# Gate and value products by Strassen's scheme, over four token blocks of 264

## The chip, the cores and the metric

The kernel runs on one core of a Trainium2 chip. Its engines each follow their own instruction stream: the tensor engine (PE in the profile, with its weight loads as PEld), the vector engine (DVE), the scalar engine (ACT), GpSimd (POOL) and the sync engine (SP), whose queue issues most of the loads from memory. The metric is the device time of one execution in microseconds (us). Before the change it is 2893.56 us, the median of three runs from 2892.72 to 2894.1.

## The reference

One layer of a decoder runs over 1024 prompt tokens and 32 sample tokens (8 sequences of 4), 1056 tokens together, with a model width of 1024. A conditioning vector gives nine modulation vectors (shift, scale and gate for each of three parts). The layer is a feed-forward network, a mixer (gated delta heads beside latent attention heads), and a second feed-forward network:

```python
def swiglu_ffn(h, wi, wo):
    gate, up = jnp.split(h @ wi, 2, axis=-1)
    return (jax.nn.silu(gate) * up) @ wo
...
    h = rms_norm(x, lp['norm_ffn1']) * (1 + mods[:, 1]) + mods[:, 0]
    x = x + 0.5 * mods[:, 2] * swiglu_ffn(h, lp['ffn1_wi'], lp['ffn1_wo'])
    h = rms_norm(x, lp['norm_mix']) * (1 + mods[:, 4]) + mods[:, 3]
...
    mix = jnp.concatenate([gdn_out, mla_out.astype(gdn_out.dtype)], axis=-1) @ lp['w_out']
    x = x + mods[:, 5] * mix
    h = rms_norm(x, lp['norm_ffn2']) * (1 + mods[:, 7]) + mods[:, 6]
    x = x + 0.5 * mods[:, 8] * swiglu_ffn(h, lp['ffn2_wi'], lp['ffn2_wo'])
```

The hidden width D_FF is 2816, which is 22 tiles of 128. The matrix wi holds the gate columns and, behind them, the value columns (the second half, called "up" in the reference). All data is float32.

## The kernel before, in words

Tokens stand in the columns, features in the 128 partitions. The 1056 tokens are cut into three blocks of 352 columns; the last block ends with the 32 sample tokens. Every float32 operand of a large product is split into two parts, hi and lo, and a product is three matmuls into one accumulator (`mm3`, lines 114 to 118: weight hi by activation hi, weight hi by activation lo, weight lo by activation hi; L116, L117, L118 in the profile). The hi part is a cast on ACT (L97 for weights), the lo part a subtraction on POOL or DVE (L100).

A feed-forward network (`ffn`, L354 to L405) works in chunks of two of the 22 hidden tiles. `up` of one hidden tile loads its 128 gate columns and its 128 value columns (512 KB each, through the SP queue into three buffers `wraw`), splits them, and for each token block runs 8 steps of the inner dimension times 3 matmuls for the gate and as many for the value: 3 x 2 x 24 = 144 matmuls of 352 columns, tile `pg`, two buffers of two banks. ACT takes the silu of the gate (L373), DVE multiplies it with the value (L375), ACT casts (L377), DVE subtracts (L378): the result is `ahl`. `down` of a chunk takes 3 blocks x 8 output tiles x 6 = 144 matmuls into `po`, and DVE adds each `po`, times the gate modulation, to the resident x (`residual`, L345; for the 32 sample tokens, whose modulation differs by sequence, two more small instructions, L349 and L351, in the last block). `down` of one chunk stands between the two `up`s of the next. All weights of a network are loaded and split once.

Each engine runs its instructions in the order in which they stand in its program, and a scheduler decides that order when the kernel is built, from its own model of the times. An instruction whose input is late holds everything behind it on its engine. Split weights go through eight buffers (`w`).

`norm_apply` makes hi and lo of the normalised, modulated x for one block. `load_x` brings x in and transposes it, `ada` computes modulation vectors, and `mixer_out` is the mixer's output product, followed by the norm of the second network.

## Time and profile before

| | |
|---|---|
| time, median of three runs | 2893.56 us (2892.72 to 2894.1) |
| the profiled execution's own time | 2880.28 us |
| its span, first to last instruction | 2878.3 us |
| mean granted clock of the tensor engine | 0.971 |
| PE busy | 2745.4 us, 95% of the span |
| PEld busy | 2527.9 us, 88% |
| DVE busy | 1586.6 us, 55% |
| ACT busy | 916.9 us, 32% |
| POOL busy | 803.8 us, 28% |
| loads of wi, of wo (512 KB each) | 88, 44 |

The first network's products run from about 58 us to between 800 and 900 us of the span, the mixer from there to about 2100 us, the second network from there to the end. A busy share says how long an engine had something in work, not whether the end waited for it: the chain of waits and the stage tables of the trace tell that. Matmuls overlap in their pipeline, so the time that one costs is the distance from its start to the start of the next, not its own duration. In the rows of the trace, an instruction group stands as line, engine, operation, output<-input, shapes and count, then busy us, mean ns of one, and the idle time ahead of it with what ended it.

### The profile page before, as it was taken

What the parts mean: (1) busy time and instruction counts of PE and PEld (TensorE: products, weight loads), DVE (VectorE), ACT (ScalarE), POOL (GpSimd) and SP (SyncE); (2) the same over time, 40 slices, a digit from 0 to 9 for tenths busy, and PEclk for the clock granted to TensorE, in tenths of its full rate; (3) what the DMA queues carried; (4) which work ended last, traced back from release to release, by engine and by line L of the source; (5) the groups of instructions that cost most, each with busy time, mean ns of one, the idle gap of its engine ahead of it and who ended that gap; (6) DMA issues with size and microseconds to landing.
All of it is one profiled execution on the core that took longest, in us unless ns stands there. A gap on an engine that the chain in (4) does not pass through costs nothing.

```text
span 2878.3 us, 45708 instructions
## 1 busy us (share of the span) xinstructions
PE 2745.4 (95%) x18596; PEld 2527.9 (88%) x18596; DVE 1586.6 (55%) x3260; ACT 916.9 (32%) x1674; POOL 803.8 (28%) x624
## 2 busy tenths in 40 slices
PE   6999999999999898889999988888999999999999
PEld 4899999999998788888877866666999999999998
DVE  6233333333356669977766768887364343344445
ACT  4211111111124544426666654444241111111111
POOL 3111111111123354463443556540231111111110
PEclk7999999999999999989999999997999999999999
DMA  7432322311122384551221243313211111111111
GB/s 256 128 93 88 103 87 91 90 42 52 45 70 77 114 218 135 168 171 25 69 51 48 56 114 88 89 49 106 75 52 45 45 45 45 44 52 52 45 37 61
DMA packets 286171, 238.78 MB, mean 83 GB/s; under 512 B 89390, under 2 KB 248870, under 8 KB 285192
## 3 DMA queue, kind: packets, MB, share of 16 engines
q1 hardware_dynamic: 276408, 207.54, 24.6%
q0 software_dynamic: 6144, 20.98, 2.2%
q10 hardware_dynamic: 3408, 7.33, 0.8%
q8 instruction: 147, 2.41, 0.3%
q14 instruction: 64, 0.52, 0.1%
HBM read 192.66 MB, written 43.15 MB: 82 GB/s over the span
## 4 chain that ended last, share of the span: by engine, by line
PE 43%; DVE 7%; issue 5%; POOL 4%; DMA 2%; ACT 1%; POOLq 0%; DVEq 0%; ACTq 0%; SPq 0%
PE pg L116 6%; PE pg L118 6%; PE pg L117 6%; PE po L116 4%; PE po L117 4%; PE po L118 4%; POOL gt L1353 2%; PE kraw L116 1%; PE kraw L118 1%; PE kraw L117 1%; POOL gS L1353 1%; PE pS L116 1%; DVE kss L1829 1%; PE pS L117 1%; PE pS L118 1%
## 5 line engine op out<-in xcount | busy, mean ns | idle before, releaser
L116 PE MATMUL pg<-hhi,whi 128*128 128x352 f32 x2112 | 685.3, 325 | 1.5 <-ACT hhi L333 1.5
L118 PE MATMUL pg<-hhi,wlo 128*128 128x352 f32 x2112 | 681.3, 323 | 0.0
L117 PE MATMUL pg<-hlo,whi 128*128 128x352 f32 x2112 | 679.9, 322 | 0.2 <-POOL hlo L334 0.2
L345 DVE SCALAR_TENSOR_TENSOR x<-po,modT,x 128x352 f32<-128x352 f32 (+1 forms) x552 | 314.0, 572 | 564.6 <-PE po L118 559.9
L100 POOL TENSOR_TENSOR wlo<-wraw,whi 128x1024 fp32r<-128x1024 f32 x93 | 226.1, 2436 | 1339.1 <-ACT whi L97 1148.6
L116 PEld LDWEIGHTS pg<-hhi,whi 128*128 128x128 f32 x2112 | 397.0, 188 | 21.9 <-issue 20.1
L117 PEld LDWEIGHTS pg<-hlo,whi 128*128 128x128 f32 x2112 | 398.4, 189 | 4.0 <-issue 3.4
L118 PEld LDWEIGHTS pg<-hhi,wlo 128*128 128x128 f32 x2112 | 397.0, 188 | 1.7 <-issue 1.7
L116 PE MATMUL po<-ahl,whi 128*128 128x352 f32 x1056 | 344.1, 326 | 3.1 <-DVE rt L349 1.1
L117 PE MATMUL po<-ahl,whi 128*128 128x352 f32 x1056 | 341.1, 323 | 0.0
L118 PE MATMUL po<-ahl,wlo 128*128 128x352 f32 x1056 | 340.0, 322 | 0.0
L97 ACT CAST whi<-wraw 128x1024 fp32r<-128x1024 f32 x140 | 145.3, 1049 | 528.3 <-PE po L117 285.3
L375 DVE TENSOR_TENSOR fa<-fs,pg 128x352 f32<-128x352 f32 x132 | 68.4, 519 | 324.8 <-ACT fs L373 324.7
L1829 DVE TENSOR_REDUCE kss<-ksq 128x8 f32<-128x512 f32 x256 | 173.3, 681 | 73.8 <-ACT ksq L1828 71.8
L373 ACT ACTIVATE fs<-pg 128x352 f32<-128x352 f32 x132 | 61.0, 462 | 459.9 <-PE pg L118 459.4
L116 PEld LDWEIGHTS po<-ahl,whi 128*128 128x128 f32 x1056 | 198.5, 188 | 8.4 <-issue 3.8
L1828 ACT ACTIVATE ksq<-kraw 128x512 f32<-128x512 f32 x256 | 152.1, 598 | 159.8 <-PE kraw L118 122.2
L117 PEld LDWEIGHTS po<-ahl,whi 128*128 128x128 f32 x1056 | 200.3, 190 | 0.0
L118 PEld LDWEIGHTS po<-ahl,wlo 128*128 128x128 f32 x1056 | 199.2, 189 | 0.0
L116 PE MATMUL pp<-hhi,whi 128*128 128x352 f32 (+1 forms) x576 | 191.9, 334 | 6.0 <-ACT hhi L333 2.3
L117 PE MATMUL pp<-hlo,whi 128*128 128x352 f32 (+1 forms) x576 | 190.9, 332 | 2.5 <-DVE hlo L337 1.4
L118 PE MATMUL pp<-hhi,wlo 128*128 128x352 f32 (+1 forms) x576 | 191.7, 335 | 1.5 <-POOL tss L728 1.5
(491 smaller groups left out, 4893.4 us busy)
## 6 DMA issues: line engine op xcount, KB each, us to landing
wraw<-ffn_wi SPq DMA_DIRECT2D x88, 512.0 KB
adaw<-ada_w SPq DMA_DIRECT2D x72, 512.0 KB
wraw<-ffn_wo SPq DMA_DIRECT2D x44, 512.0 KB
wraw<-w_in SPq DMA_DIRECT2D x23, 512.0 KB
x_d<-x SPq DMA_DIRECT2D x3, 1408.0 KB
x<-x_d SPq DMA_DIRECT2D x3, 1408.0 KB
dml<-dm_d SPq DMA_DIRECT2D x8, 512.0 KB
wraw<-w_out SPq DMA_DIRECT2D x8, 512.0 KB
```

The lines of the kernel that those rows point to most:

```text
L97: nc.scalar.copy(hi, raw)
L100: eng.tensor_tensor(out=lo, in0=raw, in1=f(hi), op=ALU.subtract)
L116: nc.tensor.matmul(out, whi, ahi, start=first, stop=False)
L117: nc.tensor.matmul(out, whi, alo, start=False, stop=False)
L118: nc.tensor.matmul(out, wlo, ahi, start=False, stop=last)
L345: nc.vector.scalar_tensor_tensor(out=x[:, d, :n], in0=ps[:, :n], scalar=self.modT[:, m, d, 0:1], in1=x[:, d, :n], op0=ALU.mult, op1=ALU.add)
L373: nc.scalar.activation(s, pg[:, 0, :BW], AF.Silu)
L375: nc.vector.tensor_tensor(out=a, in0=s, in1=pg[:, 1, :BW], op=ALU.mult)
L1353: mul = lambda out, a, b, op=ALU.mult: nc.gpsimd.tensor_tensor(out=out, in0=a, in1=b, op=op)
L1828: nc.scalar.activation(sq, kr, AF.Square)
L1829: nc.vector.tensor_reduce(out=ss[:, (j * 4 + m) * H:(j * 4 + m + 1) * H], in_=sq.rearrange("p (h d) -> p h d", h=H), axis=AX.X, op=ALU.add)
```

## The change

The tokens are cut into four blocks of 264 columns. Each network runs over all hidden tiles for blocks 0 and 1, then again for blocks 2 and 3; the weights are therefore loaded, combined and split twice.

For one hidden tile and a pair of token blocks, the gate and value products are a product of 2 x 2 blocks: A11 and A12 are the gate columns for the lower and upper half of the inner dimension, A21 and A22 the value columns; B11 and B21 are the two halves of the activations of the first block, B12 and B22 those of the second. The 8 block products are replaced by the 7 of the table `PRODUCTS` (Strassen's scheme in Winograd's form), each of 4 steps times 3 matmuls: 84 matmuls of 264 columns for a hidden tile and pair. `ffn_weights` makes the seven weight forms (A11, S3, S2, A12, S1, A22, S4) from the loaded columns by four sums and seven splits: for a hidden tile and pass, 7 casts on ACT, 6 instructions of 512 elements on DVE and 5 on POOL. `operands` makes the seven activation forms of a pair from the staged, normalised x (`staged`); the forms of the second pair of the first network are made while the first pair's last two `down`s run. `ffn_up` runs the products in four PSUM banks, X, Y, Z and W, and combines them on ACT and DVE: the first product in X is copied out (s1), then X collects the fourth product too; u2 = s1 + Y, u3 = u2 + Z, and the gates and values follow. `down` takes 2 blocks x 8 x 6 = 96 matmuls of 264 columns, its `po` alternating over the tags B, Y, B, X.

The matmuls through `mm3` go from 6336 (`pg`) + 3744 (`po`) + 1728 (`pp`, the mixer's input product) = 11808 of 352 columns to 7392 (X, Y, Z, W) + 4992 + 2304 = 14688 of 264 columns. In all, DVE's instructions go from 3260 to 4213, ACT's from 1681 to 2407, POOL's from 624 to 1145; loads of wi from 88 to 176, of wo from 44 to 88. The attention's small weight `wuk` is split at the mixer's start instead of at the kernel's; x of blocks 2 and 3 comes through the SP queue.

```diff
--- before.py
+++ after.py
@@ constants @@
-NB = 3
+NB = 4
 BW = NT // NB
...
+TAGS = (("lo1", "hi2", "lo2", "hi3", "lo3", "e0", "e1"), ("hi3", "e1", "e2", "e0", "lo0", "hi0", "lo1"))
+STAGE = 60.0
+PRODUCTS = (("B11", "A11", "X", False), ("T3", "S3", "Z", False), ("T2", "S2", "Y", False), ("B21", "A12", "X", True),
+            ("T1", "S1", "W", False), ("T4", "A22", "Z", True), ("B22", "S4", "W", True))
@@ class Kernel @@
...
+    def halve(self, hi, lo, src, eng):
+        self.nc.scalar.copy(hi, src)
+        eng.tensor_tensor(out=lo, in0=src, in1=f(hi), op=ALU.subtract)
+    def staged(self, p, places, mscale, mshift, ps):
+        self.stage = {}
+        for n, (b, t) in enumerate(zip((2 * p, 2 * p + 1), places)):
+            rb = self.norm_rows(b, ps)
+            for g in range(2):
+                self.stage[f"B{g + 1}{n + 1}"] = t[:, g]
+                self.normed(t[:, g], b, g, rb, mscale, mshift)
+                yield
+    def operands(self, tags):
+        nc = self.nc
+        F = self.forms = {x: self.slot(t, [P, 2, 4, BW], F32R, x) for (x, *_), t in zip(PRODUCTS, tags)}
+        q = self.stage
+        def done(n, at, eng):
+            self.halve(F[n][:, 0], F[n][:, 1], q[at], eng)
+        def minus(out, a, b):
+            nc.vector.tensor_tensor(out=q[out], in0=q[a], in1=q[b], op=ALU.subtract)
+        done("B11", "B11", nc.vector)
+        yield
+        minus("B11", "B12", "B11")
+        minus("B12", "B22", "B12")
+        yield
+        done("T3", "B12", nc.gpsimd)
+        yield
+        minus("B12", "B22", "B11")
+        yield
+        done("T2", "B12", nc.vector)
+        yield
+        done("B21", "B21", nc.gpsimd)
+        yield
+        minus("B21", "B21", "B12")
+        yield
+        done("T1", "B11", nc.vector)
+        yield
+        done("T4", "B21", nc.gpsimd)
+        yield
+        done("B22", "B22", nc.vector)
+        yield
 
...
-    def ffn(self, wi, wo, mgate, tp, ps, each, hook=lambda us: None, banks="B"):
+    def ffn_weights(self, wi, ff):
+        nc = self.nc
+        F = wi.shape[1] // 2
+        g = self.load_cols(wi, ff * P, P)
+        u = self.load_cols(wi, F + ff * P, P)
+        A11, A12, A21, A22 = g[:, 0:4], g[:, 4:8], u[:, 0:4], u[:, 4:8]
+        W = {}
+        def part(n, src, eng):
+            t = W[n] = self.wsp.tile([P, 2, 4, P], F32R, tag="w", name=n, bufs=self.wbufs)
+            self.halve(t[:, 0], t[:, 1], src, eng)
+        def tt(eng, out, a, b, op=ALU.subtract):
+            eng.tensor_tensor(out=out, in0=a, in1=b, op=op)
+        part("A11", A11, nc.gpsimd)
+        tt(nc.vector, A21, A11, A21)
+        part("S3", A21, nc.vector)
+        tt(nc.vector, A21, A22, A21)
+        part("S2", A21, nc.vector)
+        part("A12", A12, nc.gpsimd)
+        tt(nc.gpsimd, A11, A21, A11, ALU.add)
+        part("S1", A11, nc.gpsimd)
+        part("A22", A22, nc.gpsimd)
+        tt(nc.vector, A12, A12, A21)
+        part("S4", A12, nc.vector)
+        return W
+    def ffn_up(self, W, act, tp, ps, hook):
+        nc = self.nc
+        B = {n: ps.tile([P, 512], F32, tag=n, name="p" + n)[:, 0:BW] for n in "XZYW"}
+        T = lambda n, w, bufs: tp.tile([P, w], F32, tag=n, name=n, bufs=bufs)
+        tt = lambda out, a, b, op=ALU.add: nc.vector.tensor_tensor(out=out, in0=a, in1=b, op=op)
+        sg, cc = T("sg", 2 * BW, 2), T("cc", 2 * BW, 2)
+        for n, (x, w, bank, add) in enumerate(PRODUCTS):
+            for k in range(4):
+                self.mm3(B[bank], W[w][:, 0, k], W[w][:, 1, k], self.forms[x][:, 0, k], self.forms[x][:, 1, k], k == 0 and not add, k == 3 and (add or bank == "Y"),
+                         skip_group_check=True)
+            if n == 0:
+                s1 = T("s1", BW, 1)
+                nc.scalar.copy(s1, B["X"])
+            elif n == 2:
+                u2, u3 = T("u2", BW, 2), T("u3", BW, 2)
+                tt(u2, s1, B["Y"])
+                tt(u3, u2, B["Z"])
+            elif n == 3:
+                nc.scalar.activation(sg[:, :BW], B["X"], AF.Silu)
+            elif n == 4:
+                tt(cc[:, BW:], u3, B["W"])
+            elif n == 5:
+                tt(cc[:, :BW], u2, B["Z"])
+            elif n == 6:
+                tt(u3, u2, B["W"])
+                nc.scalar.activation(sg[:, BW:], u3, AF.Silu)
+            hook(1.45)
+        tt(cc, sg, cc, ALU.mult)
+        nc.scalar.copy(act[:, 0], cc)
+        nc.gpsimd.tensor_tensor(out=act[:, 1], in0=cc, in1=f(act[:, 0]), op=ALU.subtract)
+    def ffn(self, wi, wo, mgate, tp, ps, acts, tags, each, late, hook=lambda us: None, banks="B"):
 
         nc = self.nc
         nf = wo.shape[0] // P
...
+        turn, self.wcount = 0, 0
+        chunks = [range(c, min(c + CH, nf)) for c in range(0, nf, CH)]
+        def down(p, chunk, act, each=None, side=None):
+            ws = [self.split(self.load_rows(wo, ff * P), (D,)) for ff in chunk]
+            for b in (2 * p, 2 * p + 1):
+                c = slice(b % 2 * BW, b % 2 * BW + BW)
                 for d in range(KT):
                     po = ps.tile([P, 512], F32, tag=banks[d % len(banks)], name="po")
-                    for n, (ff, act) in enumerate(chunk):
+                    for n in range(len(chunk)):
                         self.mm3(po[:, :BW], ws[n][0][:, d * P:(d + 1) * P], ws[n][1][:, d * P:(d + 1) * P],
-                                 act[b][:, 0], act[b][:, 1], n == 0, n == len(chunk) - 1)
+                                 act[:, n, 0, c], act[:, n, 1, c], n == 0, n == len(chunk) - 1)
                     self.residual(b, d, mgate, po, tp)
-                    hook(0.45 * len(chunk))
-                    if last:
+                    hook(0.36 * len(chunk))
+                    if each:
                         each(b, d)
...
+        for p in range(2):
+            prev = None
+            for c in chunks:
+                act = self.slot(acts[turn % 2], [P, CH, 2, 2 * BW], F32R, "act")
+                turn += 1
+                last = c is chunks[-1]
+                self.ffn_up(self.ffn_weights(wi, c[0]), act[:, 0], tp, ps, hook)
+                if prev and not last:
+                    down(p, *prev)
+                for n, ff in enumerate(c[1:]):
+                    self.ffn_up(self.ffn_weights(wi, ff), act[:, 1 + n], tp, ps, hook)
+                if last:
+                    side = late() if p else self.operands(tags)
+                    down(p, *prev, side=side)
+                    down(p, c, act, each, side)
+                    for _ in side:
+                        pass
+                prev = c, act
 
@@ def mixer_out @@
-        for b in range(NB):
...
+        side = iter(())
+        for p in range(2):
             for n, w in enumerate(ws):
-                product(b, KT - 3 + n, w)
-                self.norm_squares(b, tn, *((KT - 4, 2), (KT - 2, 1), (KT - 1, 1))[n], nc.vector)
-                if b and n == 0:
-                    self.norm_sums([b - 1], tn, ps)
-                    self.norm_apply(b - 1, 7, 6, tn, ps, NB - 1)
-        self.norm_sums([NB - 1], tn, ps)
-        self.norm_apply(NB - 1, 7, 6, tn, ps, NB - 1)
+            self.norm_sums([2 * p, 2 * p + 1], tn, ps)
+            if not p:
+                side = operands()
+        for _ in side:
+            pass
@@ def body @@
...
+    def banks(e, name):
+        pool = lambda t, n: e.enter_context(tc.tile_pool(reuse_waits="tile", name=name + t, bufs=n, space=PSUM))
+        return Banks(**{t: pool(t, n) for t, n in (("X", 1), ("Y", 1), ("Z", 1), ("W", 1), ("B", 2), ("C", 2))})
...
+                    k.load_x((0, 1), ("hi0", "lo0", "hi1"), ps, nc.scalar)
+                    k.small_vectors(tp, ps, "C")
+                    for b in (0, 1):
+                        k.norm_squares(b, tn, eng=(nc.gpsimd, nc.vector)[b])
+                    k.norm_sums((0, 1), tn, ps)
+                    k.key_tables(tp, ps, "C")
+                    run(k.ada(0, 2, tp, ps, "C", ("lo1", "hi2", "lo2", "hi3", "lo3", "e0", "e1", "e2")))
+                    run(k.staged(0, places("lo0", "hi1"), 1, 0, ps))
+                    run(k.operands(TAGS[0]))
+                    k.load_x((2, 3), ("hi0", "e2", "lo0"), ps, nc.sync)
...
+                        for b in (2, 3):
+                            k.norm_squares(b, tn)
+                            yield
+                        k.norm_sums((2, 3), tn, ps)
+                        yield from k.staged(1, places("lo0", "hi1"), 1, 0, ps)
+                        for m in (3, 5, 7):
...
-                        k.ffn(ins["ffn1_wi"][0], ins["ffn1_wo"][0], 2, tp, ps, each, hook)
+                    k.ffn(ins["ffn1_wi"][0], ins["ffn1_wo"][0], 2, tp, ps, ("e2", "hi0"), TAGS[0], each, late, hook, "BYBX")
...
+                    bg, credit = k.staged(1, places("hi2", "lo3"), 7, 6, ps), [0.0]
-                    k.ffn(ins["ffn2_wi"][0], ins["ffn2_wo"][0], 8, tp, ps, finished, banks=POT[0])
+                    k.ffn(ins["ffn2_wi"][0], ins["ffn2_wo"][0], 8, tp, ps, ("hi1", "lo2"), TAGS[1], finished, lambda: iter(()), hook, "BYBX")```

DVE in the second network before, around the end of an `up` and the start of a `down` (fa and ahl are the products of an `up`, x0 is token block 0, wlo a split weight):

```order
L375 TENSOR_TENSOR fa_26955<-fs_26953,pg_26904 128x352 [waits Activation_49]
L378 TENSOR_TENSOR ahl_26957<-fa_26955,ahl_26957 128x352 [waits Activation_49]
L345 SCALAR_TENSOR_TENSOR x0_20194<-po_27028,modT_62,x0_20194 128x352 [waits PE_49]
L100 TENSOR_TENSOR wlo_27253<-wraw_27250,whi_27252 128x1024 [waits DMAHW6_49,Activation_49]
L375 TENSOR_TENSOR fa_27011<-fs_27009,pg_26960 128x352 [waits Activation_49]
L345 SCALAR_TENSOR_TENSOR x0_20194<-po_27036,modT_62,x0_20194 128x352 [waits PE_49]
```

DVE after, at the same kind of place, first pass of the second network (wraw_27026 is the value column block of the next hidden tile, DMAHW a load's semaphore):

```order
L447 TENSOR_TENSOR u3_26825<-u2_26824,pW_26783 128x264 [waits DVE_49,PE_49]
L428 TENSOR_TENSOR wraw_27026<-wraw_27024,wraw_27026 128x512 [waits DMAHW6_49,DMAHW7_49,DMAHW4_49,Pool_49]
L447 TENSOR_TENSOR cc_26785<-sg_26784,cc_26785 128x528 [waits Activation_49]
L405 SCALAR_TENSOR_TENSOR x0_23649<-po_26896,modT_62,x0_23649 128x264 [waits PE_49]
L405 SCALAR_TENSOR_TENSOR x0_23649<-po_26904,modT_62,x0_23649 128x264 [waits PE_49]
L405 SCALAR_TENSOR_TENSOR x0_23649<-po_26912,modT_62,x0_23649 128x264 [waits PE_49]
L405 SCALAR_TENSOR_TENSOR x0_23649<-po_26920,modT_62,x0_23649 128x264 [waits PE_49]
L340 TENSOR_TENSOR S3_27032<-wraw_27026,S3_27032 128x512 [waits Activation_49]
```

Before, a weight's lo part stood between residuals; now the first sum of the next hidden tile's weights, which waits for loads and for POOL, stands ahead of the multiplication that ends the `up` and of the residuals of `down`.

PE after, between the products of one hidden tile (tile X takes B11 by A11, then B21 by A12, then Z takes T4 by A22), in the order that 36 of the 88 `up`s have; in the others between 12 and 36 matmuls of other products stand between the two products in X:

```order
L117 MATMUL pX_33052<-B11_29072,A11_33027 128x264
L118 MATMUL pX_33052<-B11_29072,A11_33027 128x264
L116 MATMUL pX_33052<-B21_29075,A12_33038 128x264 [waits Activation_49]
L117 MATMUL pX_33052<-B21_29075,A12_33038 128x264
...
L118 MATMUL pX_33052<-B21_29075,A12_33038 128x264
L116 MATMUL pZ_33053<-T4_29077,A22_33045 128x264 [waits DVE_49]
```

Before, the two accumulations of `pg` had no instruction of another engine between them; now the second product in X waits for ACT's copy of the first.

POOL after, around the change from one hidden tile's weights to the next (act is the lo part of an `up`'s result):

```order
L340 TENSOR_TENSOR A22_27046<-wraw_27026,A22_27046 128x512 [waits Activation_49]
L340 TENSOR_TENSOR A11_27162<-wraw_27158,A11_27162 128x512 [waits DMAHW0_49,Activation_49]
L428 TENSOR_TENSOR wraw_27158<-wraw_27160,wraw_27158 128x512 [waits DMAHW1_49,DMAHW5_49,DVE_49,Pool_49]
L340 TENSOR_TENSOR A12_27173<-wraw_27158,A12_27173 128x512 [waits PE_49,Activation_49]
L340 TENSOR_TENSOR S1_27177<-wraw_27158,S1_27177 128x512 [waits PE_49,Activation_49]
L340 TENSOR_TENSOR A22_27180<-wraw_27160,A22_27180 128x512 [waits PE_49,Activation_49]
L472 TENSOR_TENSOR act_26750<-cc_27058,act_26750 128x528 [waits Activation_49]
```

POOL's sum in place (L428) waits for DVE's subtraction from the same buffer, and the lo part that `down` needs (act) stands behind the five weight instructions.

321 lines of the change are left out of this document (144 added, 177 removed).

## The prediction

> **What bounds the kernel now.** I read the page first: busy shares, the chain of waits, and the costliest groups.
>
> ```profile
> PE 2745.4 (95%) x18596; PEld 2527.9 (88%) x18596; DVE 1586.6 (55%) x3260; ACT 916.9 (32%) x1674; POOL 803.8 (28%) x624
> ...
> PE 43%; DVE 7%; issue 5%; POOL 4%; DMA 2%; ACT 1%; POOLq 0%; DVEq 0%; ACTq 0%; SPq 0%
> ...
> L116 PE MATMUL pg<-hhi,whi 128*128 128x352 f32 x2112 | 685.3, 325 | 1.5 <-ACT hhi L333 1.5
> ...
> L345 DVE SCALAR_TENSOR_TENSOR x<-po,modT,x 128x352 f32<-128x352 f32 (+1 forms) x552 | 314.0, 572 | 564.6 <-PE po L118 559.9
> L100 POOL TENSOR_TENSOR wlo<-wraw,whi 128x1024 fp32r<-128x1024 f32 x93 | 226.1, 2436 | 1339.1 <-ACT whi L97 1148.6
> ```
>
> PE has hardly any idle time ahead of its gate and value products (1.5 us in 2112), while DVE waits 564.6 us for `po` and POOL 1339.1 us mostly for ACT's casts. Then the stage tables (columns: stretch, its length, busy time and count of PE, PEld, DVE, ACT, POOL, granted clock, DMA share, GB/s):
>
> ```profile
> 2300.00:2500.00 200.00, 200.00 (x1256) 200.00 (x1255) 83.63 (x160) 34.15 (x52) 28.70 (x12) 1.00 0.15 46
> ...
> 780.00:900.00 120.00, 111.81 (x679) 105.31 (x678) 75.32 (x178) 39.40 (x66) 37.44 (x30) 0.97 0.26 83
> 900.00:1000.00 100.00, 94.56 (x587) 86.87 (x585) 55.82 (x119) 44.28 (x93) 33.92 (x28) 1.00 0.25 75
> ```
>
> Inside a network PE is never idle: 200.00 / 1256 = 159.2 ns for each matmul of 352 columns, and this alone sets the time. The change gains what its matmuls take less, and loses every wait that it gives PE.
>
> **a. The matmuls.** No row has 264 columns. The nearest are the attention's:
>
> ```profile
> 1652.58 0.28 PE L117 MATMUL pa<-plo,vhi 128*128 128x128 f32 x1
> 1652.69 0.28 PE L118 MATMUL pa<-phi,vlo 128*128 128x128 f32 x1
> ...
> 1652.97 0.28 PE L117 MATMUL pa<-plo,vhi 128*128 128x256 f32 x1
> 1653.09 0.28 PE L118 MATMUL pa<-phi,vlo 128*128 128x256 f32 x1
> 1653.21 0.28 PE L116 MATMUL pT<-qk,qk 104*128 104x256 f32 x1
> ```
>
> From start to start, 256 columns take 0.12 us, and 128 columns 0.11, a floor. Between 256 and 352 columns the slope is (159.2 - 120) / 96 = 0.41 ns a column, so 264 take about 0.121 (0.119 to 0.124, since the rows have two digits). 14688 x 0.121 = 1777 us replace 11808 x 0.1592 = 1880: **-103** (-132 to -59). By parts: `up` 7392 x 0.121 - 6336 x 0.1592 = -114, `po` (`down` and the mixer's output) 4992 against 3744 = +8, the mixer's input 2304 against 1728 = +4, since a narrower matmul costs a little more for each column. The Trainium skill (TensorE: Matmul & The Clock Gate, Back-to-back issue gap) gives an isolated gap of columns / 2.4 + 2.5 ns; that would be an estimated 112.5 ns at 264 and a gain of 228 us, but the same formula has 149 ns at 352, where the trace has 159.2.
>
> I call one `down` and two `up`s of a pair a **round**: 264 x 0.121 = 31.9 us of PE; the same share of work takes 34.4 before (216 x 0.1592). There are 44 rounds, 40 of them with a `down` between `up`s.
>
> **b. The copy of X.** In 36 of 88 `up`s the second product in X follows directly on the first, and waits until ACT has copied it.
>
> ```profile
> 2410.51 0.32 PE L118 MATMUL pg<-hhi,wlo 128*128 128x352 f32 x1
> 2410.93 0.47 ACT L373 ACTIVATE fs<-pg 128x352 f32<-128x352 f32 x1 [0.30 <-PE pg L118]
> ...
> 2419.61 0.49 ACT L377 CAST ahl<-fa 128x352 fp32r<-128x352 f32 x1 [0.59 <-DVE fa L375]
> ...
> 2420.13 0.52 DVE L378 TENSOR_TENSOR ahl<-fa,ahl 128x352 fp32r<-128x352 f32 x1 [0.55 <-ACT ahl L377]
> ...
> L373 ACT ACTIVATE fs<-pg 128x352 f32<-128x352 f32 x132 | 61.0, 462 | 459.9 <-PE pg L118 459.4
> L1524 ACT ACTIVATE pf<-pT 128x512 f32<-128x512 f32 x48 | 28.5, 598 | 15.5 <-PE pT L118 11.5 <-DVE qk L1467 2.1 <-POOL plo L1528 1.8
> ```
>
> ACT starts 0.10 us after a matmul ends (2410.83 to 2410.93), and the next engine 0.03 us after ACT (2420.10 to 2420.13). A matmul of 264 columns ends about 0.28 us after its start, 0.16 later than its successor could begin; the copy takes 0.462 - 88 x 0.00085 = 0.39 us; with both handovers that is 0.68 us, times 36 = **+25** (14, if only the copy counts, to 25). In the other `up`s, 12 or more matmuls (1.45 us) lie between.
>
> **c. Weights late at the start of a `down`.** Weight work doubles, and per hidden tile it is now a chain over three engines:
>
> ```profile
> 363.26 0.38 SPq L106 DMA_DIRECT2D wraw<-ffn_wi  x1
> ...
> 367.13 1.05 ACT L97 CAST whi<-wraw 128x1024 fp32r<-128x1024 f32 x1 [2.98 <-DMA wraw<-ffn_wi]
> ...
> L1528 POOL TENSOR_TENSOR plo<-pf,phi 128x512 fp32r<-128x512 f32 x48 | 61.9, 1295 | 102.4 <-ACT phi L1527 94.6 <-PE pss L118 6.1 <-PE pT L1522 1.2
> L1527 ACT CAST phi<-pf 128x512 fp32r<-128x512 f32 x48 | 29.8, 622 | 0.9
> L1808 DVE TENSOR_TENSOR klo<-kpt,khi 128x512 fp32r<-128x512 f32 x64 | 43.8, 685 | 6.6 <-ACT khi L1807 6.0
> ```
>
> A load takes 3.8 us from issue to use; an instruction of 512 elements 1.30 us on POOL, 0.62 on ACT, 0.69 on DVE. Three `wraw` buffers turn: the value columns of a tile go where the tile before had its gate columns, free only when that tile's S4 is split, and S4's own `w` buffer comes free only when the `down` ends. Counted from that end:
>
> - S4 split: three casts and a subtraction behind them, 2.9 us;
> - load 3.8;
> - on DVE and ACT the difference, S3's cast and subtraction, the next difference: 0.69 + 0.62 + 0.69 + 0.69 = 2.7;
> - POOL's run, its sum and the lo parts of A12, S1 and A22 (4 x 1.30), act (528 elements, 1.33) and one wo (L100, 2.44): 9.0;
> - the next load into the buffer that this wo had: 3.8;
> - DVE's difference on it, which stands ahead of the multiplication and the residuals of the next `down`: 0.7, then 1.2 until the first residual is done.
>
> This is 24.1 us. PE meanwhile has two `up`s (20.3) and the four `po` buffers of the new `down` (4 x 0.73 = 2.9): 23.2. So PE waits 0.9 us, if nothing meets. But DVE and POOL disturb each other:
>
> ```profile
> 2413.20 1.72 DVE L378 TENSOR_TENSOR ahl<-fa,ahl 128x352 fp32r<-128x352 f32 x1 [0.55 <-ACT ahl L377]
> ...
> 2409.76 4.76 POOL L100 TENSOR_TENSOR wlo<-wraw,whi 128x1024 fp32r<-128x1024 f32 x2 [30.05 <-ACT whi L97]
> ```
>
> The same instruction takes 1.72 us beside a running POOL instruction, and 0.52 without (b's row). One such meeting in the chain (1.2 us, of which waits for ACT cover some 0.4) makes 1.7 us: x 40 = **+68**. None and a faster load (0) to more than two meetings (3.5) gives 0 to 140. What covers the chain is PE's own work; without that cover the chain would cost all of its 24 us a round.
>
> **d. The samples' block.** In the second pass DVE does three instructions for each `po` of the last block:
>
> ```profile
> 2403.51 0.55 DVE L345 SCALAR_TENSOR_TENSOR x<-po,modT,x 128x320 f32<-128x320 f32 x1
> ...
> 2404.47 0.55 DVE L345 SCALAR_TENSOR_TENSOR x<-po,modT,x 128x320 f32<-128x320 f32 x1
> ...
> L345 DVE SCALAR_TENSOR_TENSOR x<-po,modT,x 128x352 f32<-128x352 f32 x368 | 212.9, 583 | 427.6 <-PE po L118 427.5
> L345 DVE SCALAR_TENSOR_TENSOR x<-po,modT,x 128x320 f32<-128x320 f32 x184 | 101.1, 550 | 137.0 <-PE po L118 132.4
> L351 DVE TENSOR_TENSOR x<-x,rt 128x32 f32<-128x32 f32 x184 | 71.4, 390 | 5.1
> ```
>
> The three repeat every 0.96 us at 320 columns, so about 0.87 at 232 (1.03 ns a column from the two L345 rows), against PE's 0.73 for a `po`; before, PE had 0.96 too. L351 takes 390 ns on the mean, because it meets POOL; with POOL about twice as busy I add 0.4 for each. Eight `po`s fall behind by 8 x 0.54 = 4.3 us; four buffers hide 2.9, and the one that PE waits for takes its own 0.4: 1.8 us, x 20 `down`s = **+36** (0, if POOL is quiet then, to 20 x 4.0 = 80).
>
> **e. Edges.** At the change of pair DVE has eight instructions of 1056 elements for the new forms (8 x 1.4 from L1808 scaled) and 32 residuals (32 x 0.49): 27 us, against 192 matmuls = 23.2 us: +5 in each network with the first product's wait. At the start and behind the mixer's output I put 5 and 6 for the forms that PE waits for, and 4 for norms in shorter pieces: **+25** (0 to 50). PE's start is already loose, as this row shows:
>
> ```profile
> 0.00:58.00 58.00, 35.56 (x188) 18.84 (x188) 31.07 (x59) 18.80 (x24) 20.26 (x21) 0.71 0.89 299
> ```
>
> **Sum:** -103 + 25 + 68 + 36 + 25 = **+51**, on the profiled execution's 2880.28: 2931. That execution lies 13.3 us below the median of the runs, so the forecast is **2945 us**.
>
> **Rivals.** R1, *the weights come in time*: c and d vanish, -103 + 25 + 25 = -53, 2841 us, faster. For it: POOL now works 28.7 of 200 us in a network, and c without a meeting is only 0.9 us, d without POOL's meetings nothing. Against it: POOL's work per round rises to 10 x 1.30 + 2 x 1.33 + 1.33 x 2.44 = 18.9 us of 32. It decides below 53 / 40 = 1.3 us for a round, c and d together.
>
> R2, *DVE becomes the bound*, by these rows and L345's:
>
> ```profile
> L375 DVE TENSOR_TENSOR fa<-fs,pg 128x352 f32<-128x352 f32 x132 | 68.4, 519 | 324.8 <-ACT fs L373 324.7
> L100 DVE TENSOR_TENSOR wlo<-wraw,whi 128x1024 fp32r<-128x1024 f32 x47 | 57.4, 1220 | 42.1 <-ACT whi L97 41.9
> ```
>
> Per round 16 residuals x 0.49 = 7.9, ten sums of 264 x 0.43 and two products of 528 x 0.70 = 5.7, twelve weight instructions x 0.69 = 8.3, two thirds of one wo at 1.22 = 0.8: 22.7 us, and for the samples 8 x 0.37 in the second pass, 1.5 on the mean. Of these, 14.7 have both inputs in SBUF; if four in five of them wait 1.2 us for POOL, that is 14.1 more, 38.3 us a round against 34.4: 44 x 3.9 + 25 = +197, **3090 us**; it decides from about half of them on. That DVE can starve for longer is in the trace:
>
> ```profile
> 1639.29 3.91 DVE L531 TENSOR_TENSOR pv<-rsk 128x128 f32<-128x128 f32 x1
> ...
> 1639.13 1.43 POOL L1500 TENSOR_TENSOR mix<-rl,rc 64x352 f32<-64x352 f32 x2
> 1640.52 2.53 POOL L1528 TENSOR_TENSOR plo<-pf,phi 128x512 fp32r<-128x512 f32 x2
> ```
>
> Against it: ten of the sums read PSUM and L375, which reads PSUM, shows no such wait in its mean of 519 ns. The Trainium skill (SBUF — State Buffer, Who interferes with whom) says that only a DVE instruction with two SBUF inputs contends with a GpSimd instruction that reads SBUF, and that the later one blocks entirely; the 1.72 us agrees.
>
> R3, *PE's clock*: short waits in each round lower the granted clock to the 0.97 of the stretch from 780 to 900 us: 1405 x 0.03 = +42, **2987 us**. Against it: from 900 to 1000 us PE was idle for 5% and kept 1.00. [...]
>
> **Chances.** Forecast 0.44 (its own range 2895 to 3000), R1 0.33, R2 0.08, R3 0.09, and 0.06 for a balance within 0.2%, about what a measurement of this kernel can tell from no change. Faster 0.34 (R1 and a tail), same 0.06, slower 0.60. The range takes in most of R1 and R3 and leaves R2 out: 2825 to 3030.
>
> **What would show it.** a: starts 0.12 us apart within a product. b: idle ahead of PE's X products, released by ACT's copy, 36 times about 0.6 us. c: idle ahead of `po` products released by DVE's residual, behind a DVE difference that a load released. d: the same in the second pass only, with L351's successor stretched. R2 would show DVE busy for over 90% of a round, R3 a granted clock under 1.00 within a network. I am wrong if PE is idle for less than 1.2 us a round (then faster), or if the matmuls stand 0.13 us apart (then 132 us slower than summed).

## The result and the profile after

After the change the kernel takes 3214.27 us (median of four runs, 3210.24 to 3222.25) for 2893.83 us before (median of four runs beside them, 2892.72 to 2894.65): a ratio of 1.1111, 95% interval 1.1085 to 1.1137. The forecast was 2945 us with a range to 3030: the sign was right, the size far off. The profiled execution took 3210.26 us, its span is 3208.5 us, 330.2 longer than before.

The page of the kernel after: busy shares, the chain by engine, and the groups of the weights' work on POOL and DVE.

```profile
PE 2802.3 (87%) x21560; PEld 2532.0 (79%) x21560; DVE 2244.0 (70%) x4212; ACT 1286.6 (40%) x2399; POOL 1544.9 (48%) x1143
...
PE 32%; DVE 26%; DMA 15%; POOL 13%; issue 9%; ACT 5%; SPq 0%; DVEq 0%; ACTq 0%; POOLq 0%
...
L340 POOL TENSOR_TENSOR A<-wraw,A 128x512 fp32r<-128x512 f32 x264 | 407.3, 1546 | 308.7 <-ACT A L339 301.1
...
L428 DVE TENSOR_TENSOR wraw<-wraw 128x512 f32<-128x512 f32 x264 | 276.8, 1048 | 198.8 <-DMA wraw<-ffn_wi 163.0
...
L340 DVE TENSOR_TENSOR S<-wraw,S 128x512 fp32r<-128x512 f32 x264 | 266.6, 1010 | 58.5 <-ACT S L339 57.7
...
L428 POOL TENSOR_TENSOR wraw<-wraw 128x512 f32<-128x512 f32 x88 | 114.4, 1300 | 353.5 <-DVE wraw L428 288.8
```

PE is no longer the chain: DVE, loads and POOL together hold 54% of it, 13% before. POOL's lo parts of the A forms take 1.55 us where 1.30 was summed (its sum takes the 1.30), and DVE's weight instructions 1.05 and 1.01 where 0.69 was. DVE waits 163 us for loads of wi.

Where the time went, by stage. The bounds are starts of matmuls in the trace: the first product of a network, its last `po`, the last `pp` of the mixer's input, the first and last `po` of the mixer's output. All in us.

| | start | network 1 | mixer input | heads | mixer output | network 2 | tail | span |
|---|---|---|---|---|---|---|---|---|
| before | 57.9 | 814.6 | 410.5 | 722.3 | 96.3 | 769.5 | 7.1 | 2878.3 |
| after | 92.2 | 901.1 | 446.2 | 741.1 | 99.8 | 915.3 | 12.8 | 3208.5 |
| difference | 34.3 | 86.5 | 35.7 | 18.8 | 3.5 | 145.8 | 5.7 | 330.2 |

Each network has a steady part and edges. This table gives the time from start to start of a network's matmuls, in ns for each (bare, as in undisturbed stretches: 159.2 before, 121.5 after), for the first 5% of them, the next 40%, the middle 10% (the change of pair after), the next 40% and the last 5%.

| | first 5% | 40% | middle 10% | 40% | last 5% |
|---|---|---|---|---|---|
| before, network 1 | 200 | 173 | 173 | 162 | 199 |
| before, network 2 | 171 | 160 | 160 | 160 | 198 |
| after, network 1 | 142 | 160 | 189 | 141 | 177 |
| after, network 2 | 232 | 144 | 226 | 143 | 169 |

The stage table of the kernel after, for a steady stretch of network 2 (stretch, length, PE, PEld, DVE, ACT, POOL with counts, granted clock, DMA share, GB/s):

```profile
2380.00:2460.00 80.00, 70.55 (x534) 67.20 (x532) 53.82 (x83) 26.66 (x49) 43.58 (x27) 0.98 0.27 80
```

No engine is full: PE is idle for 9.45 of 80 us, DVE works 67%, POOL 54%. The limit is a chain that goes from one to the other. This is it, the chain of waits of 2400 to 2480 us, in order of time (start, length, what):

```profile
2402.00 0.61 DVE wraw L428
2402.74 1.15 POOL wraw L428
2403.99 0.75 POOL A L340
...
2405.70 1.36 POOL S L340
...
2407.42 1.75 POOL A L340
2409.17 1.74 POOL act L472
2410.91 2.36 POOL wlo L100
2413.29 4.58 DMA wraw<-ffn_wi
2417.99 0.93 DVE wraw L428
2418.98 0.63 ACT S L339
2419.65 0.59 PE pZ L116
...
2433.51 1.38 DVE S L340
2434.95 3.98 DMA wraw<-ffn_wi
2439.05 0.70 DVE wraw L428
...
2443.96 1.79 DVE cc L447
2445.76 1.71 DVE wraw L428
...
2449.51 1.94 DVE wlo L100
2451.47 5.41 DMA wraw<-ffn_wi
2456.98 1.78 DVE wraw L428
```

It is the chain that term c described, link by link: sum, POOL's run, act, wo, the load into the freed buffer, DVE's difference. But POOL's run from 2402.74 to 2413.27 takes 10.5 us for 9.0, the loads 4.0 to 5.4 for 3.8, and DVE's difference up to 1.8 for 0.7. PE meets it at two places, at the residuals and at `pZ`, the product with S3. Its waits in network 1, then in network 2 (line, what it waited for: us, times, longest):

```profile
PE po L116 <- DVE x L405: 31.0, 15, 5.9
...
PE pZ L116 <- ACT S L339: 7.2, 4, 2.5
```

```profile
PE pZ L116 <- ACT S L339: 25.8, 15, 2.2
PE po L116 <- DVE x L405: 17.6, 9, 11.2
```

### The profile page after: what moved, and what is told of

It reads as the page before. It is cut to its first block, busy times and chain, and to the rows that moved or that the text cites. A ratio compares the mean times of both kernels' runs of the same rounds, so it can differ in the third digit from the quotient of the medians.

```text
span 3208.5 us, 54936 instructions
## 1 busy us (share of the span) xinstructions
PE 2802.3 (87%) x21560; PEld 2532.0 (79%) x21560; DVE 2244.0 (70%) x4212; ACT 1286.6 (40%) x2399; POOL 1544.9 (48%) x1143
## 4 chain that ended last, share of the span: by engine, by line
PE 32%; DVE 26%; DMA 15%; POOL 13%; issue 9%; ACT 5%; SPq 0%; DVEq 0%; ACTq 0%; POOLq 0%
DMA wraw<-ffn_wi 10%; DVE wraw L428 5%; PE po L116 4%; PE po L117 4%; PE po L118 3%; DVE S L340 3%; POOL A L340 3%; POOL wlo L100 2%; ACT S L339 2%; DVE cc L447 2%; POOL gt L1449 2%; POOL wraw L428 1%; DVE cy L820 1%; PE pp L116 1%; PE pp L118 1%
## 5 line engine op out<-in xcount | busy, mean ns | idle before, releaser
L340 POOL TENSOR_TENSOR A<-wraw,A 128x512 fp32r<-128x512 f32 x264 | 407.3, 1546 | 308.7 <-ACT A L339 301.1
L116 PE MATMUL po<-act,whi 128*128 128x264 f32 x1408 | 419.5, 303 | 65.6 <-DVE x L405 48.6
L405 DVE SCALAR_TENSOR_TENSOR x<-po,modT,x 128x264 f32<-128x264 f32 (+1 forms) x736 | 334.7, 477 | 136.5 <-PE po L118 134.5
L339 ACT CAST S<-wraw 128x512 fp32r<-128x512 f32 x352 | 218.2, 620 | 512.6 <-DVE wraw L428 426.7
L428 DVE TENSOR_TENSOR wraw<-wraw 128x512 f32<-128x512 f32 x264 | 276.8, 1048 | 198.8 <-DMA wraw<-ffn_wi 163.0
L118 PE MATMUL po<-act,wlo 128*128 128x264 f32 x1408 | 394.4, 295 | 20.2 <-POOL wlo L100 16.9
L117 PE MATMUL po<-act,whi 128*128 128x264 f32 x1408 | 407.3, 293 | 0.0
L116 PEld LDWEIGHTS po<-act,whi 128*128 128x128 f32 x1408 | 277.2, 197 | 98.3 <-DVE x L405 64.2
L340 DVE TENSOR_TENSOR S<-wraw,S 128x512 fp32r<-128x512 f32 x264 | 266.6, 1010 | 58.5 <-ACT S L339 57.7
L118 PEld LDWEIGHTS po<-act,wlo 128*128 128x128 f32 x1408 | 269.6, 198 | 28.0 <-POOL wlo L100 22.9
L428 POOL TENSOR_TENSOR wraw<-wraw 128x512 f32<-128x512 f32 x88 | 114.4, 1300 | 353.5 <-DVE wraw L428 288.8
L117 PEld LDWEIGHTS po<-act,whi 128*128 128x128 f32 x1408 | 276.7, 197 | 0.0
L339 ACT CAST A<-wraw 128x512 fp32r<-128x512 f32 x264 | 162.9, 617 | 264.4 <-PE po L117 121.0
L116 PE MATMUL pX<-B,A 128*128 128x264 f32 x704 | 209.3, 297 | 42.9 <-ACT s L455 20.4
L100 POOL TENSOR_TENSOR wlo<-wraw,whi 128x1024 fp32r<-128x1024 f32 x63 | 159.8, 2538 | 152.9 <-ACT whi L97 147.3
L117 PE MATMUL pp<-hlo,whi 128*128 128x264 f32 (+1 forms) x768 | 226.3, 295 | 3.7 <-DVE hlo L340 3.7
L116 PE MATMUL pp<-hhi,whi 128*128 128x264 f32 (+1 forms) x768 | 226.9, 296 | 2.0 <-ACT hhi L339 2.0
L118 PE MATMUL pp<-hhi,wlo 128*128 128x264 f32 (+1 forms) x768 | 224.2, 293 | 0.4 <-POOL wlo L581 0.4
L118 PE MATMUL pX<-B,A 128*128 128x264 f32 x704 | 203.1, 288 | 1.2 <-POOL A L340 1.2
L117 PE MATMUL pX<-B,A 128*128 128x264 f32 x704 | 203.3, 289 | 0.3 <-DVE B L340 0.3
```

What stands on the lines that cost most here:

```text
L100: eng.tensor_tensor(out=lo, in0=raw, in1=f(hi), op=ALU.subtract)
L116: nc.tensor.matmul(out, whi, ahi, start=first, stop=False, **kw)
L117: nc.tensor.matmul(out, whi, alo, start=False, stop=False, **kw)
L118: nc.tensor.matmul(out, wlo, ahi, start=False, stop=last, **kw)
L339: self.nc.scalar.copy(hi, src)
L340: eng.tensor_tensor(out=lo, in0=src, in1=f(hi), op=ALU.subtract)
```

## The experiments

Each kernel was timed once, in the execution that was profiled, except the last; the kernel before took 2891 to 2904 us beside them. Stages in us from the traces:

| | start | network 1 | mixer, three stages | network 2 | tail | span |
|---|---|---|---|---|---|---|
| before | 57.9 | 814.6 | 1229.1 | 769.5 | 7.1 | 2878.3 |
| four blocks, no Strassen, one pass | 68.4 | 829.5 | 1268.0 | 802.6 | 6.6 | 2975.2 |
| two passes, no Strassen | 78.9 | 818.7 | 1280.0 | 798.7 | 13.3 | 2989.5 |
| after | 92.2 | 901.1 | 1287.1 | 915.3 | 12.8 | 3208.5 |
| POOL's lo parts left out | 88.6 | 810.0 | 1274.7 | 796.1 | 12.9 | 2982.2 |
| five load buffers in network 2 | 91.8 | 897.5 | 1285.7 | 829.9 | 10.9 | 3115.7 |
| ten split buffers in network 2 | 91.8 | 903.3 | 1299.3 | 852.2 | 12.8 | 3159.5 |
| POOL's weight work on DVE | 92.2 | 823.9 | 1293.0 | 811.6 | 12.7 | 3033.4 |
| the same, and five load buffers | 92.7 | 823.3 | 1277.4 | 793.9 | 11.1 | 2998.5 |
| lo parts left out, five load buffers | 87.5 | 810.3 | 1278.4 | 784.6 | 11.1 | 2971.8 |
| four forms made for seven | 76.7 | 895.5 | 1293.9 | 896.8 | 12.7 | 3175.6 |
| POOL's weight and form work on DVE | 91.4 | 822.7 | 1284.2 | 811.6 | 12.8 | 3022.8 |
| the same, and five load buffers | 90.6 | 825.0 | 1277.7 | 791.1 | 11.3 | 2995.7 |

The mixer tells how far one execution can be trusted: of the edits of the kernel after, the nine that keep Strassen leave the mixer's own instructions as they are, and it took 1274.7 to 1299.3 us in them. Differences of some 12 us in a mixer, or in a span, are not taken for effects here.

**Strassen alone undone.**

```diff
+PLAIN = (("B11", "A11", "X", False), ("B21", "A12", "X", True), ("B12", "A11", "Z", False), ("B22", "A12", "Z", True),
+         ("B11", "A21", "Y", False), ("B21", "A22", "Y", True), ("B12", "A21", "W", False), ("B22", "A22", "W", True))
...
         part("A11", A11, nc.gpsimd)
-        tt(nc.vector, A21, A11, A21)
-        part("S3", A21, nc.vector)
...
+        part("A12", A12, nc.vector)
+        part("A21", A21, nc.gpsimd)
+        part("A22", A22, nc.vector)
```

> Strassen alone is undone: four blocks of 264 and two passes stay, but a hidden tile and pair takes the eight plain block products (96 matmuls for 84), its weights are split in four halves without sums, and the activation forms are four for seven. Theory 1 (the chain that makes the seven weight forms, loads and two engines in turn, is what PE waits for): the chain is short here, so the networks take little more than their matmuls, 12672 x 0.122 = 1546 us and about 100 at the edges, for 1816 after: a span of about 3040 us. Rival (loading and splitting all weights twice is the cost, with or without sums): the networks stay at 1800 us or more, a span of 3200 us.

The span is 2989.5 us: 219 less, with 1056 matmuls more. A steady stretch of its network 2:

```profile
2300.00:2400.00 100.00, 100.00 (x825) 100.00 (x825) 41.04 (x69) 27.84 (x48) 34.50 (x22) 1.00 0.31 96
```

PE is never idle and the clock is 1.00, at 100.00 / 825 = 121.2 ns for each matmul. So in this stretch, weights that are loaded and split twice cost nothing, and 264 columns take what the forecast said; both networks together take 1617 us, 15 less than with four blocks and one pass (below). The rival falls; what costs is Strassen's own work, on the forms of weights and activations and on the sums of the products, which this run undoes all at once. Against this kernel, Strassen saves 1056 x 0.1215 = 128 us of matmuls and is 219 us slower, so it pays 347 us, 327 of them in the networks.

**POOL's lo parts of weights left out.**

```diff
         def part(n, src, eng):
...
-            self.halve(t[:, 0], t[:, 1], src, eng)
+            if eng is nc.gpsimd:
+                nc.scalar.copy(t[:, 0], src)
+            else:
+                self.halve(t[:, 0], t[:, 1], src, eng)
...
-                self.mm3(B[bank], W[w][:, 0, k], W[w][:, 1, k], self.forms[x][:, 0, k], self.forms[x][:, 1, k], k == 0 and not add, k == 3 and (add or bank == "Y"),
+                self.mm3(B[bank], W[w][:, 0, k], W[w][:, int(w in ('S2', 'S3', 'S4')), k], self.forms[x][:, 0, k], self.forms[x][:, 1, k], k == 0 and not add, k == 3 and (add or bank == "Y"),
```

> The four lo parts of weights that POOL makes for each hidden tile (A11, A12, S1, A22) are left out, and the hi part is multiplied in their place; all matmuls, loads, casts and DVE's instructions stay. Theory 1 (chain): POOL's run between two loads loses 4 x 1.5 us, so the steady rounds fall from 38.3 us to about 33. Theory 2 (DVE and POOL disturb each other): DVE's weight instructions fall from a mean of 1.05 us toward 0.69. If both hold, the networks lose some 200 of 1816 us, a span of about 3000 us; if neither is the cause (PE's rate or DVE's own work), the span stays above 3150 us.

The networks lose 210 of 1816 us, as expected if both theories hold: four instructions of a hidden tile are worth 60% of the 347 us. DVE's weight instructions fall from 1.05 and 1.01 us to 0.77 and 0.86, not all the way to 0.69; POOL's sum, act and wo are left. How much is POOL's shorter run and how much the disturbance, this run does not tell.

**Five load buffers in the second network.**

```diff
-        self.wraw = e.enter_context(self.tc.tile_pool(reuse_waits="tile", name="wraw", bufs=3))
+        self.wraw = e.enter_context(self.tc.tile_pool(reuse_waits="tile", name="wraw", bufs=raw))
...
-        with k.weights(), k.residents(), k.extra(), ExitStack() as pse:
+        with k.weights(5, 8), k.residents(), k.extra(), ExitStack() as pse:
```

> In the second network alone there are five buffers for loaded weights, not three. Theory 1 with the loads as its core: the value columns of the next tiles need not wait for the tile before, the 85 us that DVE waits for loads there mostly vanish, and the second network goes from 915 us to about 850. Theory 2 (disturbance between DVE and POOL) or a bound by their work: 915 us less 15 at most. The first network and the mixer stay.

Network 2 goes from 915.3 to 829.9 us, with every instruction of the engines kept. The waits of DVE in network 2, after and here (engine, line, what it waited for: us, times, longest):

```profile
DVE wraw L428 <- DMA wraw<-ffn_wi: 84.6, 40, 9.0
```

```profile
DVE wraw L429 <- DMA wraw<-ffn_wi: 49.2, 30, 7.4
```

85 us come back, as expected if the loads are at the core. The wait for loads does not vanish, and loads of wi still hold 100 us of network 2's chain of waits, for 182 in the kernel after. The first network keeps its three buffers, and stays (897.5 us for 901.1).

**Four blocks alone.** The kernel before with `NB = 4`, and only what four blocks need to fit.

```diff
-NB = 3
+NB = 4
...
-            for cb, n in ((0, P), (P, P), (2 * P, BW - 2 * P)):
+            for cb, n in ((0, 88), (88, 88), (176, 88)):
```

> The kernel before with four blocks of 264 for three of 352, and nothing else of the change: one pass, plain products, weights loaded and split once. By term a the networks take 12672 x 0.122 = 1546 us for 1584 before (with waits), the mixer 8 more. Theory 3 (the mixer's 55 us and the later start come from the narrower blocks, whose pieces cost DVE more): the mixer goes from 1229 to about 1280 us here too. Rival (they come from the staged forms, the order of loads and the split of wuk at the mixer's start): the mixer stays within 15 us of before, and the first product starts near 58 us.

The mixer takes 1268 us, 39 more, and the span is 96.9 us longer than before. Theory 3 holds as far as one execution can tell: most of the mixer's 58 us come with the narrower blocks (the start gives 10). PE's waits in the mixer's input, before, here, and after:

```profile
PE pch L758 <- DVE tok L742: 6.0, 2, 4.4
```

```profile
PE pch L758 <- DVE tok L742: 26.1, 6, 7.2
```

```profile
PE pch L861 <- DVE tok L845: 24.1, 6, 6.2
```

The waits for DVE's `tok` grow fourfold with the narrower blocks alone. More work on DVE is not the reason: it has 16 `tok` instructions in both kernels and is busy for 318 us of the mixer's input, 322 before. Why they come later for PE stays open.

**POOL's five weight instructions on DVE**, in both networks: `nc.vector` for `nc.gpsimd` in the four `part`s and the one sum.

```diff
-        part("A11", A11, nc.gpsimd)
+        part("A11", A11, nc.vector)
...
-        tt(nc.gpsimd, A11, A21, A11, ALU.add)
+        tt(nc.vector, A11, A21, A11, ALU.add)
```

> POOL's five instructions for the weights of a hidden tile (the lo parts of A11, A12, S1, A22 and the sum for S1) are done by DVE; POOL keeps act and two thirds of wo. Theory 2 (DVE and POOL disturb each other) and theory 1 (POOL's run lies in the chain): DVE's weight instructions fall from 1.05 us to about 0.7, five instructions of 0.7 replace a run of five of 1.5, and the networks fall from 1816 us by 100 or more. Rival (DVE is the bound): its work per round rises from about 27 us, stretched, to 31 unstretched against 32 of PE, DVE is busy over 95% of a round, and the networks stay at 1800 us or more.

The networks fall by 181 us, although DVE has 440 instructions more. The groups in network 2 of the kernel after, then of this one from 2280 us on, 71 us behind the network's start (busy, mean ns):

```profile
L428 DVE TENSOR_TENSOR wraw<-wraw 128x512 f32<-128x512 f32 x129 | 138.8, 1076 | 99.0 <-DMA wraw<-ffn_wi 84.6 <-POOL A L340 10.5 <-POOL wlo L100 3.5
...
L340 DVE TENSOR_TENSOR S<-wraw,S 128x512 fp32r<-128x512 f32 x130 | 136.7, 1052 | 33.7 <-ACT S L339 33.6
...
L405 DVE SCALAR_TENSOR_TENSOR x<-po,modT,x 128x264 f32<-128x264 f32 x264 | 119.4, 484 | 33.2 <-PE po L118 32.9
...
L411 DVE TENSOR_TENSOR x<-x,rt 128x32 f32<-128x32 f32 x88 | 24.6, 281 | 1.1
```

```profile
L340 DVE TENSOR_TENSOR S<-wraw,S 128x512 fp32r<-128x512 f32 x161 | 113.4, 704 | 10.5 <-ACT S L339 9.4
L405 DVE SCALAR_TENSOR_TENSOR x<-po,modT,x 128x264 f32<-128x264 f32 x252 | 113.3, 484 | 11.7 <-PE po L118 11.2
L428 DVE TENSOR_TENSOR wraw<-wraw 128x512 f32<-128x512 f32 x160 | 112.6, 703 | 32.7 <-DMA wraw<-ffn_wi 30.8
...
L340 DVE TENSOR_TENSOR A<-wraw,A 128x512 fp32r<-128x512 f32 x120 | 89.3, 744 | 31.2 <-ACT A L339 30.8
```

The same instructions take 0.70 us where they took 1.05 to 1.08, while the residual, which reads PSUM, takes 484 ns in both. So the 0.35 us are the disturbance by POOL. What it is worth, this run does not part from the shorter run (five instructions of 0.7 for five of 1.5): both go at once. The Trainium skill (SBUF — State Buffer, Who interferes with whom) names two SBUF inputs as the condition for a DVE instruction outside its 2-port perf modes, and the two groups agree.

**Ten split buffers, and two combinations.** `k.weights(3, 10)` in the second network; then DVE for POOL with five load buffers; then the lo parts left out with five load buffers.

> In the second network alone ten buffers for split weights stand in place of eight, the loads keep their three. If the chain is held where S4's split waits for a split buffer that comes free at the end of a down, the second network falls from 915 us to under 880; if the chain is held by the three load buffers alone, it stays within 15 us of 915.

> POOL's five weight instructions on DVE in both networks, and five load buffers in the second. The second network took 830 us with five buffers alone. If what is left there is the disturbance between DVE and POOL, it falls to about 780 us; if DVE's own work is then the limit, it stays at 830 or rises. The first network should repeat the run without the buffers.

> POOL's four lo parts are left out (the hi part is multiplied in their place) in both networks, and five load buffers in the second. Alone these gave 796 and 830 us for the second network, from 915. If POOL's run and the loads are parts of one chain, either one frees it and both together give about 785 us; if they are two separate waits, the gains add to about 711, which is close to the bare matmuls (5808 x 0.1215 = 706).

Ten split buffers alone bring network 2 to 852.2, 63 us less: the wait for a split buffer, S4's among them, is a link of the chain as well. The combinations reach 793.9 and 784.6 us, not the 726 and 711 of added gains: POOL's run and the load buffers are links of one chain, and to slacken either frees much of it. The split buffers were not tried together with another. The first combination expected about 780 and is nearer to that than to 830.

**The activation forms.** Four splits and no sums in `operands`, the products with T1 to T4 taking B12's split; and, in the next run, POOL's three form splits on DVE in addition to its weight work.

> The work on the activation forms is cut to that of the plain products: four splits (B11, B12, B21, B22) and no sums; the products with T1 to T4 take B12's split in their place. Weights, matmuls and everything else stay. After the change, the middle tenth of a network's matmuls (the change of pair) took 226 ns for each in the second network and 189 in the first, for 121.5 bare. If the forms' work on DVE and POOL is what PE waits for there, this falls to about 160, and the first product starts some 8 us earlier: together about 65 us less, a span near 3145 us. Rival (stores of y that hold load buffers, and the weights' fresh start): the middle tenth stays over 205 ns and the span within 25 us of 3208.

> As the run with POOL's five weight instructions on DVE, and POOL's three lo parts of activation forms on DVE too. If the disturbance between the two engines also holds up the change of pair, whose instructions of 1056 elements took 3.4 us on DVE for 1.4 expected, the middle tenth falls from 178 ns (second network) and 151 (first) toward 150 and 135, about 25 us in all, a span near 3010 us. If DVE's own added work cancels it, the span stays within 10 us of 3033.

The start comes 15.5 us earlier, but the middle tenth of network 2 only falls from 226 to 205 ns (of network 1 from 189 to 171), and the span by 33 us, half of what was expected. To move the form splits from POOL makes no difference that one run can show (3022.8 for 3033.4, network 2 the same 811.6, the middle tenths 180 and 153 ns for 178 and 151), though the splits of T then take DVE 1.3 to 1.4 us. So the forms are a part of the cost of a change of pair, and not its larger one. The rest shows two waits: in the kernel after, DVE first waits behind POOL (first two fences: timeline of DVE and of POOL), and then the second pass's first weights wait for the stores of y, which use the load buffers (third: chain of waits):

```profile
2707.03 3.38 DVE L377 TENSOR_TENSOR st<-st 128x1056 f32<-128x1056 f32 x1 [1.64 <-POOL T L340]
2710.34 3.40 DVE L340 TENSOR_TENSOR B<-st,B 128x1056 fp32r<-128x1056 f32 x1
```

```profile
2703.55 3.44 POOL L340 TENSOR_TENSOR T<-st,T 128x1056 fp32r<-128x1056 f32 x1
```

```profile
2750.84 5.23 DMA y_prompt<-yt
2756.21 5.88 DMA wraw<-ffn_wi
2762.21 0.70 DVE wraw L428
```

With five load buffers the middle tenth of network 2 was 181 ns, which fits the rival, but with POOL's lo parts left out it was 173 and with POOL's weight work on DVE 178, with three load buffers. So the weights' chain is in it too; how the rest divides was not tried.

**All three together**, with two timed runs.

> All three changes that freed the chain together: POOL's weight and form work on DVE, five load buffers in the second network. By the single runs the span is about 2975 us. It stays slower than the kernel before, because four narrow blocks alone cost 97 us (span 2975 without Strassen) and the bare matmuls that Strassen saves against plain products are 1056 x 0.1215 = 128 us, of which the copies of X, the forms and the clock take back about that much. Rival: with the chain freed, Strassen's 128 us appear in full and the span is under 2878.

2999.38 us (2997.58 to 3001.18), a ratio of 1.0352 to the kernel before (1.0294 to 1.0409). This is 215 us better than the change as made and still slower than before; the span of 2995.7 us is 21 above what was expected. Its networks take 1616 us, those of plain products 1617: freed this far, Strassen gains in matmuls what it loses in waits, and the rival falls. No version with the four narrow blocks that ran was faster than before.

## Why the prediction was wrong, point by point

The 330 us by their places: the networks' bare matmuls, (11616 x 0.1215) - (9504 x 0.1592) = -102; the rest of their steady parts 204; of their edges (first and last 5%, middle 10%) 130; the start 34, the mixer 58, the tail 6. Of the 204 some 42, and of the 130 some 32, are matmuls at half clock (last section). The forecast had -103 (with 5 lost in the mixer), 129 for the steady parts (b, c and d) and 25 for the edges of all kinds (e), where 228 came. So two steps failed: e, far outside its own range of 0 to 50, and c, which came out twice as large.

The right sign does not bear out the sum. Four narrower blocks alone, without Strassen, made the kernel 97 us slower, and of this the forecast held only the matmuls and 4 us for norms.

**What bounds the kernel, and a: right.** PE was the only limit before. A matmul of 264 columns takes 0.12 us, as in the timeline after:

```profile
2423.36 0.28 PE L117 MATMUL po<-act,whi 128*128 128x264 f32 x1
2423.48 0.28 PE L118 MATMUL po<-act,wlo 128*128 128x264 f32 x1
```

**b: right.** In 36 `up`s the second product in X follows directly on the first, and there PE loses 24 us in all, for 25.

**c: the right chain, mis-sized; here the steady part of the forecast failed.** The step was "One such meeting in the chain (1.2 us, of which waits for ACT cover some 0.4) makes 1.7 us", or 68 us. The steady parts' 204, less the half clock's 42 and b's 24, leave an estimated 138. In fact meetings are the rule: all 528 of DVE's weight instructions average 0.34 us over 0.69, POOL's 264 lo parts of A forms 0.25 over 1.30, POOL's run takes 10.5 us for 9.0 and a load up to 5.4 for 3.8. The chain also was counted once for a round, up to the residuals, though PE needs its links at both `up`s: at `pZ` with S3 and at wo's lo part. (By the rates given there, the first link, three casts of 0.62 and a subtraction of 0.69, adds up to 2.6 us and not 2.9, which would have made c smaller still.) In network 2 a steady round has 264 x (144 - 121.5) = 5.9 us over the bare matmuls, for 0.6 + 1.5 + 0.8 = 2.9 forecast. Freed of one link, network 2 falls by 63 to 119 us, where c and d together were 52 us for each network.

**d: wrong.** The second pass is no slower than the first (143 and 144 ns in network 2, 141 and 160 in network 1). The step that failed is "with POOL about twice as busy I add 0.4 for each": the small addition (L351 before, L411 after) goes from 334 to 375 ns in network 1, and in network 2 it falls from 429 to 281.

**e: the largest miss, 228 for 25.** The start costs 34 for 5, of which the forms are about 15 (the run with four of them) and the narrower blocks 10. At PE, transposes of blocks 2 and 3, whose x comes late, also stand ahead of the first product; the chain of waits has

```profile
85.32 4.18 DMA xt<-x_prompt
...
89.55 1.43 PE pt L201 x8
...
92.44 0.29 PE pZ L116
```

The mixer costs 58 for about 8: I gave it 4 for matmuls and 4 for norms, and did not see that PE waits for DVE there, and longer with narrower blocks; the run with four blocks alone has 39 of it. The edges inside the networks cost 130 more than before (168 over the bare matmuls for 38), for 10 at the changes of pair and 6 behind the mixer's output. Here I priced the forms alone: instructions of 1056 elements took DVE up to 3.4 us where 1.4 was scaled from an undisturbed row, and four forms for seven bring the edges from 168 to 134 us. But to leave out POOL's lo parts of weights brings them to 86, and to move POOL's weight work to DVE to 100: a good half of what the edges cost goes with the weights' work of c, which e did not have there at all. The stores of y in the load buffers were not seen either; their share, and the rest of the mixer's 58 us, stay open.

**The rivals.** R1 did not come. R2's mechanism did, without its condition: DVE is disturbed as R2 said, but is busy for 70%, not 90%. The wait does not need a full engine, it only needs to lengthen a chain that is already as long as PE's work. I weighed R2 as "DVE becomes the bound" and so gave it a chance of 0.08 only. R3 came beside c, not in its place: half clock costs the networks some 74 us more than before, where R3 was priced at 42 and given 0.09. The kernel before had shown it inside R3's own stretch: from 890.9 us on its clock was at half for 3.41 us, behind two gaps of PE of 1.37 and 1.03 us. The sign for c (idle of PE behind a DVE difference that a load released) was seen, in network 1 mostly ahead of `po` as forecast, in network 2 more ahead of `pZ`.

## What to carry to other kernels

Work that is saved on the busy engine is paid for in preparation: here 128 us of matmuls against 347 us, most of it because the weight forms pass over three engines and two loads in turn. When such a chain nearly equals the cover it lies beside, price every link at its disturbed duration and ask what one more buffer would free; and put the links on the faster engine rather than share them between DVE and POOL, which was worth 181 us here, shorter instructions and less disturbance together. A narrower tile must be priced in every stage that uses it: the four blocks cost 97 us before Strassen did anything.
